# A list scheduler that counts VectorE's SBUF-only instructions and GpSimd's as exclusive, with a fixed part in each product's price

## The chip, the cores and the metric

The kernel runs on one core of a Trainium2 chip. The core has five engines with instruction streams of their own: TensorE (PE) for products, VectorE (DVE), ScalarE (ACT) and GpSimd (POOL) for elementwise work, SyncE (SP), whose queue issues all the DMAs here. The metric is the device time of one execution in microseconds, lower is better.

## The reference

One encoder layer is computed, for a prompt of 512 tokens (p) and a sample of 1024 tokens (s), 1024 features each, in float32. Cut to what matters:

```python
n = rms_norm(x, ln1_g) * (1 + sc1) + sh1
z = n @ w_in                                   # 1024 -> 2560
q, k, v, xl, gl = split(z)                     # 8 heads of 64, and 512 recurrent channels twice
att = neighbourhood_attention(rms_norm(q), rms_norm(k), v, rpb)    # 8 rows x 16 columns of a grid
xl = depthwise_conv(xl, lru_conv_w, lru_conv_b)
h = rg_lru(xl, forward) + rg_lru(xl, backward) # two linear scans over the tokens
x = x + g1 * (concat(att, h * gelu(gl)) @ w_out)
n2 = rms_norm(x, ln2_g) * (1 + sc2) + sh2
ug, uv = split(depthwise_conv(n2 @ w_up, ffn_conv_w, ffn_conv_b))  # 1024 -> 2 x 2816
x = x + g2 * ((gelu(ug) * uv) @ w_down)
```

The six modulation vectors (sh1, sc1, g1, sh2, sc2, g2) come from `silu(c) @ w_ada + b_ada`.

## The kernel before

The program is written as a recording: every call of `R.act`, `R.vec`, `R.tt`, `R.copy`, `R.mm`, `R.dma` makes an `Op` with an engine, a price in ns, the ops it depends on, and sometimes other engines that could do it (`alts`). Nothing is issued until `R.run()`. Then `_order` goes through all 14010 ops like a list scheduler: it keeps a clock for each engine, takes the engine whose next ready op can start first, gives that op a place in memory, moves the clock on by the op's price and hands the instruction out. The order of each engine's instructions, and the engine of each op that has a choice, come from the prices alone; the chip runs each engine's instructions in that order, with semaphores in between. Since all instructions are emitted from one line, nearly all rows of the profile say L351, and a tile is named by the arena that it was put in: `arena_f`, `arena_r` and `piece0` to `piece4` are SBUF memory (F as float32, R as float32r), `arena_s` holds small vectors, `bank` is a PSUM bank.

An op's key is the time by which it must start for TensorE to run without a halt; ready ops with a lower key go first. An op may be handed out only if it is less than a window (198 us of TensorE's priced work; 48 us for DMAs; other values in the up stage) ahead of the first op in program order that isn't done.

Ops with a choice are of two kinds. A copy (`act` with `either=True`, or `copy`, `ts` with `either=True`) can go to ScalarE or to DVE. A sum, difference or product of two SBUF tiles (`tt` with `pool=None`) can go to DVE or to POOL. When the engine that is free first takes such an op, `leave` asks whether another engine would be done with it sooner, its clock and the ready ops with lower keys counted in; in that question the op's own price is multiplied by a factor of the table `LEAN`, by its first engine and the engine that asks.

The stages: the norm, projections (768 rows of weights for q, k, v and the recurrence's two inputs at a time), the attention of each pair of heads and the recurrence, p first, then s; the output projection and second norm; up (`up`), each of 22 column blocks by Strassen's scheme in Winograd's form, 7 products instead of 8; down, in 5 chunks, by the same scheme. Every float32 operand of a product is split into a high part (a copy to float32r) and a low part (a difference), and a product is three (high x high, high x low, low x high). The scheme's terms (`s1` to `s4` of the left side, `t1` to `t4` of the right) are sums and differences with a choice between DVE and POOL; so are the low parts.

The recurrence's elementwise ops on a pair of heads of s have 1024 columns (`lru`): two products for each direction before the scan, one sum of the directions and one product with the gate, and two low parts of its input, all with a choice between DVE and POOL.

## Time and profile before

| | us |
|---|---|
| median of three timed runs | 1893.22 |
| lowest, highest | 1892.41, 1893.79 |
| span of the profiled execution | 1892.9 |
| TensorE busy | 1721.7 (91%) |
| VectorE busy | 1495.2 (79%) |
| ScalarE busy | 951.8 (50%) |
| GpSimd busy | 838.9 (44%) |

No other time is given for the profiled execution than its span, from the first to the last instruction. TensorE's busy time holds instructions that overlap in its pipeline and time that an instruction spent waiting inside it, so a busy TensorE is not one at its peak; a row's duration on DVE or POOL likewise holds the time that it was held up after its start. Shares over the whole span mix stages of different kinds, so the windows of single stages are of more use: on the time axis the projections and the attention lie at 0 to 640 us, the output projection and the second norm at 640 to 900, up at 800 to 1496, down at 1496 to the end, with its first sums and splits from 1443 on.

### The profile page before, as it was taken

The numbers are of one execution on the slowest core, as the hardware profiler recorded it, in microseconds if no ns is written. First come the engines' busy times: TensorE is split into PE (matmuls) and PEld (weight loads), VectorE is DVE, ScalarE is ACT, GpSimd is POOL, SyncE is SP. The second block draws the span as 40 slices with busy tenths as digits, with TensorE's granted clock in tenths as the row PEclk, the third lists the DMA queues.
The fourth block names the chain that finished last, engine by engine and source line by source line (L and its number), as shares of the span: only waits on it lengthen the run. The fifth ranks groups of instructions, "written<-read, shape, count | busy, mean of one in ns | idle before, by whom it ended". The sixth has DMA issues, their size and how long they took to land. (4 is left out here: it accounts for less than half of the span.)

```text
span 1892.9 us, 26075 instructions
## 1 busy us (share of the span) xinstructions
PE 1721.7 (91%) x8906; PEld 1416.1 (75%) x8906; DVE 1495.2 (79%) x2662; ACT 951.8 (50%) x1753; POOL 838.9 (44%) x656
## 2 busy tenths in 40 slices
PE   6987979989898899897999999999999888888978
PEld 3665767768687578797888888888887666776756
DVE  5697797897969874868767767667698998789998
ACT  3365863857676741454444444444454554243332
POOL 0364332362616321334333333333255776467874
PEclk9998989999999899998999999999999999999989
DMA  9435314040406465462122221221232331324322
GB/s 369 162 101 150 123 45 134 17 163 13 167 12 189 99 195 173 139 206 79 56 71 64 62 68 62 62 73 56 66 97 81 115 106 55 95 71 143 118 97 97
DMA packets 144695, 201.12 MB, mean 106 GB/s; under 512 B 15793, under 2 KB 83505, under 8 KB 144561
## 3 DMA queue, kind: packets, MB, share of 16 engines
q1 hardware_dynamic: 144560, 199.44, 33.2%
q8 instruction: 70, 1.15, 0.3%
q14 instruction: 65, 0.52, 0.1%
HBM read 157.97 MB, written 41.44 MB: 105 GB/s over the span
## 5 line engine op out<-in xcount | busy, mean ns | idle before, releaser
L351 PE MATMUL bank<-arena_r 128*128 128x512 f32 (+3 forms) x3487 | 859.6, 379 | 58.0 <-ACT piece0F L351 11.0
L351 PEld LDWEIGHTS bank<-arena_r 128*128 128x128 f32 (+1 forms) x3487 | 632.2, 192 | 192.3 <-issue 22.0
L351 PE MATMUL bank<-arena_r,piece0R 128*128 128x512 f32 (+3 forms) x1323 | 325.2, 346 | 8.5 <-DVE piece4F L351 4.4
L351 PEld LDWEIGHTS bank<-arena_r,piece0R 128*128 128x128 f32 (+1 forms) x1323 | 230.6, 194 | 41.5 <-issue 6.3
L351 POOL TENSOR_TENSOR arena_r<-arena_f,arena_r 128x256 fp32r<-128x256 f32 (+4 forms) x172 | 189.8, 1113 | 159.1 <-ACT arena_r L351 74.1
L351 POOL TENSOR_TENSOR arena_f<-arena_f 128x512 f32<-128x512 f32 (+5 forms) x149 | 178.9, 1207 | 99.6 <-issue 42.9
L351 ACT ACTIVATE arena_r<-arena_f 128x256 fp32r<-128x256 f32 (+4 forms) x245 | 115.0, 495 | 130.8 <-PE bank L351 77.8
L351 PE MATMUL bank<-arena_r,piece2R 128*128 128x512 f32 (+1 forms) x735 | 179.5, 335 | 0.0
L351 DVE SCALAR_TENSOR_TENSOR arena_f<-bank,arena_s,arena_f 128x255 f32<-128x255 f32 (+2 forms) x308 | 157.5, 535 | 21.2 <-ACT arena_f L351 10.5
L351 ACT ACTIVATE arena_f<-arena_f,arena_s 128x384 f32<-128x384 f32 (+2 forms) x166 | 101.7, 619 | 84.7 <-DVE arena_s L351 54.4
L351 PEld LDWEIGHTS bank<-arena_r,piece2R 128*128 128x128 f32 x735 | 126.6, 190 | 16.4 <-POOL piece2R L351 0.2
L351 PE MATMUL bank<-arena_r,piece4R 128*128 128x256 f32 (+1 forms) x453 | 137.5, 330 | 0.4 <-DVE arena_f L351 0.4
L351 DVE TENSOR_TENSOR arena_f<-arena_f 128x512 f32<-128x512 f32 (+5 forms) x148 | 134.8, 919 | 3.7 <-ACT arena_f L351 2.5
L351 DVE TENSOR_TENSOR arena_r<-arena_f,arena_r 128x256 fp32r<-128x256 f32 (+5 forms) x143 | 123.8, 882 | 6.6 <-ACT arena_r L351 2.6
L351 ACT ACTIVATE arena_f<-bank 128x512 f32<-128x512 f32 (+3 forms) x186 | 82.3, 454 | 75.1 <-DVE bank L351 36.9
L351 PE MATMUL bank<-piece0R,arena_r 128*128 128x512 f32 (+3 forms) x316 | 104.4, 398 | 2.1 <-DVE arena_s L351 2.0
L351 ACT ACTIVATE piece0R<-arena_f 128x512 fp32r<-128x512 f32 (+2 forms) x78 | 48.9, 627 | 113.1 <-PE bank L351 92.5
L351 ACT ACTIVATE arena_f<-bank,arena_s 128x512 f32<-128x512 f32 (+1 forms) x132 | 89.6, 683 | 24.5 <-PE bank L351 15.2
L351 DVE TENSOR_TENSOR bank<-bank,arena_f 128x512 f32<-128x512 f32 (+1 forms) x89 | 52.3, 589 | 51.3 <-PE bank L351 32.8
L351 PEld LDWEIGHTS bank<-arena_r,piece4R 128*128 128x128 f32 x453 | 83.5, 190 | 9.3 <-issue 0.8
L351 ACT ACTIVATE piece2R<-arena_f 128x512 fp32r<-128x512 f32 x63 | 39.8, 631 | 89.9 <-PE bank L351 77.9
L351 DVE SCALAR_TENSOR_TENSOR arena_f<-arena_f,arena_s 128x511 f32<-128x511 f32 (+3 forms) x102 | 70.9, 696 | 17.4 <-ACT arena_f L351 15.4
(432 smaller groups left out, 3214.1 us busy)
## 6 DMA issues: line engine op xcount, KB each, us to landing
arena_f<-in_w_up_dram SPq DMA_DIRECT2D x96, 256.0 KB
gd<-arena_f SPq DMA_DIRECT2D x62, 256.0 KB
piece2F<-in_ada_dram SPq DMA_DIRECT2D x18, 512.0 KB
arena_f<-in_w_qkv_dram SPq DMA_DIRECT2D x24, 384.0 KB
arena_f<-gd SPq DMA_DIRECT2D x39, 192.0 KB
piece3F<-in_ada_dram SPq DMA_DIRECT2D x14, 512.0 KB
arena_f<-gd SPq DMA_DIRECT2D x46, 128.0 KB
arena_f<-in_ada_dram SPq DMA_DIRECT2D x8, 512.0 KB
```

Source lines behind the costliest of these rows:

```text
L351: fn(**{k: (v.real() if isinstance(v, View) else v) for k, v in kw.items()})
```

## The change

Four things change in the scheduler, and nothing in what is recorded. Comments and docstrings are dropped too, so that line numbers move by a few (L351 becomes L355).

1. A clock `port` is shared by POOL and DVE. Each op gets a set `port` of the engines on which it uses the shared clock: POOL always; DVE when the op's operands are all in SBUF, but not for `tensor_reduce` and `reciprocal`. An op that is handed out to such an engine starts no sooner than `port` and moves it to its own end.
2. `leave` compares ends without factors, the `port` clock counted in on both sides; the table `LEAN` is gone.
3. A float32r product is priced `n / 2.4 + 13.5` ns, at least 109, where it was `n / 2.4 + 2.5`.
4. The windows, `LEAD`, `LAG` and the memory steps stay.

```diff
-LEAN = {("DVE", "POOL"): 0.389, ("DVE", "DVE"): 0.536, ("ACT", "ACT"): 0.611, ("ACT", "DVE"): 1.869, ("DVE", "ACT"): 1.004}
+ONE_PORT = ("tensor_reduce", "reciprocal")
...
-    def op(self, eng, cost, emit, reads, writes, aset=None, lat=0.0, also=(), alts=(), move=0.0):
+    def op(self, eng, cost, emit, reads, writes, aset=None, lat=0.0, also=(), alts=(), move=0.0, port=False):
...
+        o.port = {"POOL"} if eng == "POOL" or "POOL" in alts else set()
+        if port:
+            o.port.add("DVE")
...
-        self.op("DVE", per * n + base + (60 if ps else 0), self._emit(getattr(self.nc.vector, name), kw), reads, w, alts=alts)
+        self.op("DVE", per * n + base + (60 if ps else 0), self._emit(getattr(self.nc.vector, name), kw), reads, w, alts=alts, port=not ps and name not in ONE_PORT)
...
-            self.op("DVE", *b, [in0, in1], [out], alts={"POOL": a} if pool is None else {})
+            self.op("DVE", *b, [in0, in1], [out], alts={"POOL": a} if pool is None else {}, port=not self._ps(out, in0, in1))
...
-            cost = max(64.0, n) / 2.4 + 2.5 if rhs.ap.dtype == F32R else max(214.0, n / 0.6)
+            cost = max(max(64.0, n) / 2.4 + 13.5, 109.0) if rhs.ap.dtype == F32R else max(214.0, n / 0.6)
...
         def leave(o, e, s):
-            """Whether another engine would be done with o before e."""
+
+            own = (max(s, port) if e in o.port else s) + o.alts[e][0]
             for f, (cost, _) in o.alts.items():
                 if f != e:
                     ahead = sum(ops[p].all[f][0] for c, p, v in ready[f] if c < o.key and not stale(c, p, v, f))
-                    if max(clock[f], s) + ahead + cost < s + LEAN[o.first, e] * o.alts[e][0]:
+                    if max(clock[f], s, port if f in o.port else s) + ahead + cost < own:
                         return True
...
+            if e in o.port:
+                s = max(s, port)
+                port = s + o.cost
```

How many ops with a choice go where, by stage of the program:

| stage | copies to ScalarE / DVE before | after | two-input ops to DVE / POOL before | after |
|---|---|---|---|---|
| projections, recurrence, attention | 260 / 220 | 301 / 179 | 138 / 186 | 145 / 179 |
| output projection, second norm | 58 / 42 | 64 / 36 | 54 / 34 | 53 / 35 |
| up | 298 / 16 | 237 / 77 | 131 / 163 | 185 / 109 |
| down | 345 / 50 | 377 / 18 | 275 / 266 | 244 / 297 |

In the first stage 19 of the ops that leave POOL have 1024 columns.

The order of POOL before, at the recurrence of the first pair of heads of s. The four rows of 128x1024 are two products ahead of the scans, the sum of the directions and the product with the gate; 128x384 are biases of the attention, 4x64 low parts of its values:

```order
L351 TENSOR_TENSOR arena_f<-piece2F,arena_f 128x384 x2
L351 TENSOR_TENSOR arena_r<-piece2F,arena_r 128x4x64 x2
L351 TENSOR_TENSOR arena_f<-arena_f 128x384
L351 TENSOR_TENSOR piece4F<-piece4F 128x1024
L351 TENSOR_TENSOR piece3F<-piece3F,piece2F 128x1024
L351 TENSOR_TENSOR piece2F<-piece2F,piece4F 128x1024
L351 TENSOR_TENSOR piece2F<-piece2F 128x1024
L351 TENSOR_TENSOR piece0R<-piece4F,piece0R 128x4x64 x2
```

POOL after the change, at the same place:

```order
L355 TENSOR_TENSOR piece4F<-piece2F,arena_f 128x384 x2
L355 TENSOR_TENSOR arena_f<-piece2F,arena_f 128x384 x2
L355 TENSOR_TENSOR arena_r<-piece4F,arena_r 128x512
L355 TENSOR_TENSOR arena_f<-piece4F,arena_f 128x384
L355 TENSOR_TENSOR piece0R<-piece2F,piece0R 128x4x64 x2
L355 TENSOR_TENSOR arena_r<-arena_f,arena_r 128x768
```

And DVE after the change, there; the four SCALAR_TENSOR_TENSOR rows are two products of the recurrence and its two scans, bank rows belong to the attention:

```order
L355 SCALAR_TENSOR_TENSOR piece3F<-piece2F,piece3F 128x1024
L355 SCALAR_TENSOR_TENSOR piece2F<-piece3F,piece2F 128x1024
L355 TENSOR_TENSOR piece3F<-piece3F,piece2F 128x1024
L355 TENSOR_TENSOR piece2F<-piece2F,piece3F 128x1024
L355 SCALAR_TENSOR_TENSOR piece2F<-piece2F,piece3F 128x1024
L355 SCALAR_TENSOR_TENSOR piece3F<-piece3F,piece2F 128x1024
L355 TENSOR_TENSOR arena_r<-bank_73,arena_r 128x3x128
L355 TENSOR_TENSOR piece2F<-piece2F,piece3F 128x1024
```

The recurrence's rows of 128x1024 have gone from POOL to DVE, in a row ahead of its scans; POOL goes on with the attention's biases and the splits of the next weights.

The DMA queue (SP) before, where down begins. `gd<-arena_f` stores a finished column block of up, `in_w_down_dram` are weights of down, `arena_f<-gd` are its left operands:

```order
L351 DMA gd<-arena_f 128x512 x4
L351 DMA arena_f<-in_w_down_dram 128x512 x3
L351 DMA arena_f<-gd 128x128 x3
L351 DMA arena_f<-in_w_down_dram 128x512
L351 DMA arena_f<-gd 128x128 x9
L351 DMA gd<-arena_f 128x512 x2
L351 DMA arena_f<-gd 128x128 x12
L351 DMA arena_f<-gd 128x2x128 x2
```

And after the change:

```order
L355 DMA gd<-arena_f 128x512 x3
L355 DMA arena_f<-in_w_down_dram 128x512 x2
L355 DMA gd<-arena_f 128x512
L355 DMA arena_f<-in_w_down_dram 128x512
L355 DMA gd<-arena_f 128x512
L355 DMA arena_f<-gd 128x128 x3
L355 DMA arena_f<-in_w_down_dram 128x512
L355 DMA arena_f<-gd 128x128 x7
```

Down's loads have moved back against up's stores: 45 of them stand ahead of up's last store before, 35 after.

## Rows read from the trace of the kernel before

**Rows 1.** The page's slices: busy tenths of two engines in 40 slices.

```profile
PE   6987979989898899897999999999999888888978
DVE  5697797897969874868767767667698998789998
```

**Rows 2.** Windows by stage: length; busy us of PE, PEld, DVE, ACT, POOL; clock; DMA.

```profile
50.00:640.00 590.00, 525.23 (x2809) 417.62 (x2809) 487.98 (x1120) 373.97 (x705) 250.09 (x195) 0.95 0.35 109
640.00:900.00 260.00, 235.00 (x1326) 202.84 (x1325) 188.43 (x290) 123.44 (x203) 83.18 (x46) 0.96 0.45 144
900.00:1395.00 495.00, 493.80 (x2834) 435.28 (x2833) 348.57 (x567) 234.32 (x411) 177.47 (x123) 1.00 0.22 67
1395.00:1496.00 101.00, 91.55 (x391) 74.87 (x390) 89.85 (x161) 50.18 (x102) 61.18 (x66) 0.93 0.28 86
1496.00:1690.00 194.00, 175.11 (x738) 137.41 (x736) 163.49 (x219) 86.11 (x169) 119.43 (x105) 0.99 0.28 86
1690.00:1893.00 203.00, 165.82 (x655) 128.93 (x655) 189.57 (x225) 65.57 (x137) 142.08 (x113) 0.93 0.34 111
```

**Rows 3.** TensorE's waits in 50:640: who, for whom, us in total, times, longest.

```profile
PE bank L351 <- DVE arena_r L351: 9.0, 9, 3.6
```

**Rows 4.** Timelines of POOL, DVE and PE at 403:414: start, us, instruction, [idle before].

```profile
403.69 5.54 POOL L351 TENSOR_TENSOR arena_r<-arena_f,arena_r 128x768 fp32r<-128x768 f32 x3 [0.95 <-DMA piece4F<-vds]
...
404.76 0.81 DVE L351 TENSOR_SCALAR arena_s<-arena_s 128x16 f32<-128x16 f32 x1
405.49 2.04 DVE L351 TENSOR_SCALAR arena_f<-arena_f,arena_s 128x384 f32<-128x384 f32 x1
407.45 1.81 DVE L351 TENSOR_SCALAR arena_s<-arena_s 128x16 int32<-128x16 int32 x1
...
413.39 0.16 DVE L351 TENSOR_TENSOR arena_s<-arena_s 128x16 f32<-128x16 f32 x1
...
413.52 1.01 PE L351 MATMUL bank<-arena_r,piece0R 128*128 128x256 f32 x3 [3.55 <-DVE arena_r L351]
```

**Rows 5.** Timelines of DVE and POOL: products of the recurrence, 128x1024, in 300:420.

```profile
348.78 1.23 DVE L351 TENSOR_TENSOR piece2F<-piece2F,piece4F 128x1024 f32<-128x1024 f32 x1 [1.17 <-ACT piece2F L351]
...
370.68 3.08 DVE L351 TENSOR_TENSOR piece3F<-piece3F,piece4F 128x1024 f32<-128x1024 f32 x1
...
369.37 3.31 POOL L351 TENSOR_TENSOR piece3F<-piece3F,piece2F 128x1024 f32<-128x1024 f32 x1 [7.46 <-DVE piece3F L351]
```

**Rows 6.** Timelines of POOL and DVE in down: side by side, then each alone.

```profile
1605.36 1.47 POOL L351 TENSOR_TENSOR arena_r<-arena_f,arena_r 128x384 fp32r<-128x384 f32 x1
1606.79 1.46 POOL L351 TENSOR_TENSOR arena_f<-arena_f,piece3F 128x384 f32<-128x384 f32 x1
...
1605.88 1.50 DVE L351 TENSOR_TENSOR arena_r<-arena_f,arena_r 128x512 fp32r<-128x512 f32 x1
...
1615.42 1.01 POOL L351 TENSOR_TENSOR piece2F<-piece0F,arena_f 128x384 f32<-128x384 f32 x1 [2.03 <-DVE arena_f L351]
...
1804.66 0.68 DVE L351 TENSOR_TENSOR arena_r<-piece1F,arena_r 128x512 fp32r<-128x512 f32 x1
```

**Rows 7.** A window in the middle of up, columns as in rows 2.

```profile
1000.00:1050.00 50.00, 50.00 (x289) 44.14 (x288) 32.58 (x52) 22.96 (x40) 15.68 (x11) 1.00 0.22 66
```

**Rows 8.** Groups by form on POOL: xcount | busy us, mean ns | idle before.

```profile
L351 POOL TENSOR_TENSOR piece2F<-piece2F,piece4F 128x1024 f32<-128x1024 f32 x4 | 10.5, 2616 | 30.9 <-ACT piece2F L351 13.5 <-DVE piece2F L351 11.7 <-DVE arena_s L351 5.6
...
L351 POOL TENSOR_TENSOR arena_f<-arena_f 128x512 f32<-128x512 f32 x80 | 117.5, 1469 | 69.6 <-issue 41.2 <-DVE arena_f L351 12.6 <-DVE arena_r L351 9.4
```

**Rows 9.** Groups by form: low parts of 128x128 on POOL and on DVE.

```profile
L351 POOL TENSOR_TENSOR arena_r<-arena_f,arena_r 128x128 fp32r<-128x128 f32 x38 | 21.8, 586 | 24.4 <-DVE arena_r L351 11.5 <-ACT arena_r L351 7.4 <-DMA piece3F<-in_tab_dram 4.6
...
L351 DVE TENSOR_TENSOR arena_r<-arena_f,arena_r 128x128 fp32r<-128x128 f32 x24 | 10.0, 444 | 0.1
```

**Rows 10.** Waits in 1395:1496, columns as in rows 3.

```profile
ACT arena_f L351 <- DVE arena_f L351: 10.5, 10, 3.1
...
PE bank L351 <- ACT arena_f L351: 8.4, 2, 4.3
```

More of the change, by code (lines that the diff above doesn't have):

```diff
@@ L208 @@
 class Op:
-    __slots__ = ("pos", "eng", "cost", "lat", "emit", "deps", "left", "users", "ready", "bufs", "aset", "start", "end", "vt", "done", "name", "alts", "all", "win", "ver", "key", "first", "move", "late", "strict")
+    __slots__ = ("pos", "eng", "cost", "lat", "emit", "deps", "left", "users", "ready", "bufs", "aset", "start", "end", "vt", "done", "name", "alts", "all", "win", "ver", "key", "first", "move", "late", "strict", "port")
 class Recorder:
@@ L372, in act @@
             alts["DVE"] = (1.045 * self._n(in_) + 127 if self._ps(in_) else 0.523 * self._n(in_) + 67, self._emit(self.nc.vector.tensor_copy, dict(out=out, in_=in_)))
-        self.op("ACT", cost, self._emit(self.nc.scalar.activation, kw), [in_, scale, bias], [out, accum_out], aset=SETS.get(func), alts=alts)
+        self.op("ACT", cost, self._emit(self.nc.scalar.activation, kw), [in_, scale, bias], [out, accum_out], aset=SETS.get(func), alts=alts, port=either and not self._ps(out, in_))
     def _act(self, out, in_, scale=None):
@@ L568, in _order @@
         aset = None
-        moved = 0.0
+        moved = port = 0.0
         tick = 0
```

## The prediction

> **What bounds the kernel now.** I read the page's slices first [rows 1], then stage windows [rows 2], then TensorE's waits [rows 3], then single instructions where waits gather [rows 4 to 6]. In the slices the reader is to see three parts: TensorE at 7 to 9 tenths with VectorE (DVE) at 7 to 9 in the first third, TensorE full in the middle, and TensorE falling to 7 or 8 at the end while DVE stands at 9. The windows give them numbers [rows 2]. In 50:640 (projections, recurrence, attention) TensorE is idle for 590 - 525.23 = 65 us and its granted clock is 0.95 of full speed; DVE is busy for 487.98 us, 83%. In 900:1395 (up products) TensorE is busy for 493.80 of 495: that stretch can't be shortened by any order. In 1395:1496 it idles 9 us, in 1496:1690 19 us, in 1690:1893 37 us; there DVE is busy for 189.57 of 203 us, 93%. So order and division of work decide outside 900:1395, through DVE. TensorE's longest wait in the first stretch, summed over one pair of tiles, is for DVE [rows 3].
>
> What DVE loses is visible too. At 403.69 three GpSimd (POOL) products of 128x768 run for 5.54 us, and a DVE instruction on 128x16 takes 1.81 us in that time, where a like one takes 0.16 us later; TensorE's 3.55 us of idle end right behind [rows 4]. Two products of 128x1024 side by side end 4.39 us after the first began (369.37 to 370.68 + 3.08), where one alone on DVE takes 1.23, two in a row some 2.46 [rows 5]. In the down stage POOL and DVE take turns, POOL starting every 1.43 us [rows 6]. So these two engines shut each other out on SBUF, and a planner that prices an instruction as if it were alone divides wrongly.
>
> **The change part by part.** *TensorE's price.* A 512-column product goes from 215.8 to 226.8 ns, one of 256 from 109.2 to 120.2 (from the formulas of the diff). The up stage is half of each: the new mean is 173.5 ns, and the trace shows 50 us for 289 products, 173 ns [rows 7]. The new price is right; by itself it moves no work between engines, and it shortens the planner's look ahead by 5 to 10% of products, since its windows are not changed. I cost that at nothing on its own; it is part of the term for the down stage below.
>
> *Projections and attention (50:640).* Here 19 products of 128x1024 of the sample's recurrence go from POOL to DVE, and 12 more small ones (net) go to POOL; 41 copies (net) go from DVE to ScalarE. POOL loses 19 x 2.616 = 50 us [rows 8], 20% of its 250.09 busy us [rows 2]. DVE takes 19 x 1.23 = 23 us [rows 5] and gives up some 41 copies and 12 products of roughly half a us each, an estimate from the 0.444 us of a 128x128 product and 0.68 us of a 128x512 one [rows 6, 9]: 26 us. Its own work stays. What it saves is waiting. Beside the 5.54 us of POOL at 403.69 it waits some 3.7 us (0.81 - 0.16, 1.81 - 0.16, and 2.04 less the 0.68 of a wider product), 0.66 of it [rows 4, 6]; in front of an instruction that reads PSUM, as many of DVE's are, it waits for nothing. I take 0.4 of POOL's time for the stretch: 0.4 x 50 = 20 us back, with 0 and 33 as bounds. TensorE is not behind DVE everywhere, so I take three quarters: **-15 us** (0 to -33). ScalarE gets 41 copies, at about 0.5 us some 20 us on 374 of 590: it stays the less busy engine, and if its cover is gone the cost is those 20 us at most.
>
> That figure can be weighed against the Trainium skill, SBUF — State Buffer, Who interferes with whom: the pair of ports that VectorE and GpSimd share is a lock held for the whole instruction, and the second one fully blocks. The trace has 1.43 us for a pair whose parts alone are 0.68 and 1.01 us [rows 6], so about a quarter us overlaps, and here the measurement decides. By the page's whole lock the share would be nearer the 0.66 above, the term -25, and the sum below 1870.
>
> *640:900.* Out projection and second norm: of 188 instructions with a choice 6 more go to ScalarE and 1 more to POOL, net; TensorE idles 25 us [rows 2]. I take -2, with 6 either way.
>
> *Up, 900:1395.* 61 copies go from ScalarE to DVE and 54 products from POOL to DVE: at most 115 x 0.68 = 78 us more on DVE's 348.57, so 86% of 495 instead of 70%, while POOL gives up 54 x 1.469 = 79 us of its 177 [rows 2, 6, 8]. TensorE has no idle time to win and hides this as long as DVE keeps up: 0, and up to +10 if it does not.
>
> *The end of up, 1395:1496.* TensorE waits twice, for 8.4 us together, for ScalarE, which itself waits for DVE there [rows 10]. In this stretch the old order already does down work (below); the new one does less of it, so the stretch gets lighter: -4 (0 to -9).
>
> *The start of down, 1496:1690.* In the order in which the planner hands instructions out, 63 DVE and 50 POOL instructions of the down stage stand ahead of the last up product; after the change 11 and 21. The DMA queue says the same: 45 loads of the down stage stand ahead of up's last store before, 35 after. So 52 DVE and 29 POOL instructions move behind the last product of up, most of them 128x128: 52 x 0.444 = 23 us of DVE and 29 x 0.586 = 17 us of POOL [rows 9]. DVE is busy for 163.49 of 194 us there [rows 2], idle for 30.5. 23 us fit, and part of the 17; but at the start TensorE waits for just this work. Bounds 0 and +40; I take **+8**, nearer to the end at which idle time takes it.
>
> *The rest of down, 1690:1893.* In the whole down stage 31 products (net) go from DVE to POOL, and 32 copies from DVE to ScalarE. With DVE at 93% this looks like relief, but a POOL product keeps the ports longer than a DVE one (1.01 us for 384 columns against 0.68 for 512, [rows 6]), so what 31 DVE products free goes to waiting: 0, with 8 us either way.
>
> *Sum* against the profiled execution's own span: 1892.9 - 15 - 2 + 0 - 4 + 8 + 0 = **1880 us**. The median of the three timed runs, 1893.22, is 0.3 us from that span, so I carry the sum over as it is.
>
> **The rivals.** *Down starts cold (slower).* All 40 us of DVE and POOL work that the new order leaves behind the last up product come on top, because the ports are full in the down stage: DVE at 93% in its second half speaks for it, and that the planner, told of the ports, still gives POOL 297 of 541 products there, where it gave 266. Against it stands the 16% of idle DVE in 1496:1690. With -15 and -4 kept: 1892.9 - 19 + 40 = 1914, and 1905 if a quarter of it finds room. It decides once DVE can no longer take up the first 20 of the 40 us, that is, once it is busy for over 94% between up's last product and the middle of down.
>
> *A truer order gains more.* The term of the first stretch prices only moved instructions. Here the planner also knows that DVE is late, and puts what TensorE waits for ahead of the rest. If a third of the 65 us of idle goes and the granted clock rises with it (a mean of 0.95 with levels of 1.2 and 2.4 GHz is a tenth of the 590 us, 59 us, at the low one, which costs up to 30 us): -22 - 10 on top, 1848. For it: DVE's waits of 1 to 2 us on tiny instructions [rows 4]. Against: POOL's work there shrinks by a fifth only.
>
> *Nothing that can be measured.* The change does not do what its price says: POOL still takes most products in down, DVE's own work is the same in the first stretch, and what is won there is lost at the start of down: 1889 to 1897.
>
> **How the numbers follow.** I give the forecast (1862 to 1889) 0.40, the truer order 0.17, no change 0.13, the cold start 0.30. A measurement of this kernel tells some 0.2% from no change, 3.8 us; the cases give faster 0.57, same 0.13, slower 0.30. The range takes in the truer order's 1848 and most of the cold start: 1846 to 1912. The forecast's own range, from the bounds of its terms, is 1862 to 1889.
>
> **What would show it.** In the changed profile: no 128x1024 product of the recurrence on POOL, POOL's busy time down to some 210 us before 640 us, and the up stage's end some 15 to 20 us earlier on the time axis: right for the first term. TensorE's idle time in the first 25 to 50 us of down larger than now, and DVE near 95% there: the cold start. If TensorE is below 98% in the middle of up, DVE did not keep up there, and my 0 for that stretch is wrong. The prediction fails if the first stretch keeps its 65 us of idle, or if down loses more than 20 us.

## The result, and the profile after

The changed kernel takes 1847.1 us (median of 4 runs, 1845.4 to 1850.9) where the kernel before takes 1893.5: a ratio of 0.976, 95% interval 0.9746 to 0.9774, so 46 us less. The direction was forecast, the size was not: the forecast was 13 us less, with a range that just reaches down to the measured time. The rival that gave 1848, a truer order, had been given 17%. Of the kernel with one number changed (1840.1 us, below) one run in four took 3331.7 us, and the time given is the median of the other three.

The page of the changed kernel, against [rows 1] and the table of busy times of before; TensorE is fuller in the first tenth and behind the middle, GpSimd emptier until down begins, and DVE at 9 tenths in two of the last 13 slices where it was in six:

```profile
PE 1716.7 (93%) x8906; PEld 1411.1 (76%) x8906; DVE 1436.9 (78%) x2673; ACT 944.2 (51%) x1769; POOL 720.5 (39%) x627
...
PE   7998879899999699999999999999999889998878
...
DVE  5676878877988775878687777777787888879889
...
POOL 0244233061616200336221111111133689968877
```

To compare stage by stage, both traces are cut where TensorE has got through the same amount of work (its products, each at the new price, in the order in which they ran), at the moments that are 50, 640, 900, 1395, 1496 and 1690 us before. Windows of the changed kernel at those cuts, with the columns of [rows 2]:

```profile
47.70:609.40 561.70, 517.51 (x2810) 414.17 (x2809) 443.40 (x1066) 389.33 (x750) 211.26 (x202) 0.96 0.34 107
609.40:866.20 256.80, 238.05 (x1328) 203.26 (x1327) 189.95 (x298) 125.59 (x209) 67.08 (x41) 0.95 0.52 164
866.20:1367.80 501.60, 497.31 (x2835) 436.60 (x2833) 371.52 (x692) 202.10 (x350) 86.88 (x64) 1.00 0.22 65
1367.80:1455.60 87.80, 86.84 (x390) 71.09 (x389) 65.18 (x105) 43.40 (x82) 38.07 (x33) 1.00 0.23 72
1455.60:1649.60 194.00, 176.36 (x737) 140.18 (x736) 166.02 (x223) 103.92 (x225) 159.53 (x154) 0.96 0.34 102
1649.60:1846.90 197.30, 166.23 (x655) 127.31 (x653) 175.16 (x211) 64.29 (x134) 155.34 (x129) 0.94 0.34 113
```

The lengths of these windows less those of before, beside the terms of the forecast. At 1690 TensorE of the kernel before stands in a wait that ends at 1692.5; the table counts it to the stretch ahead of the cut, which is then 196.4 us long, and the last one 200.4:

| stage, by the times of before | forecast (bounds) | measured |
|---|---|---|
| ahead of 50 | none | -2.3 |
| 50:640 projections, recurrence, attention | -15 (0 to -33) | -28.5 |
| 640:900 output projection, norm | -2 (±6) | -3.2 |
| 900:1395 up | 0 (up to +10) | +6.5 |
| 1395:1496 end of up | -4 (0 to -9) | -13.1 |
| 1496:1690 start of down | +8 (0 to +40) | -2.4 |
| 1690 to the end | 0 (±8) | -3.1 |
| sum | -13 | -46 |

So the gain is in the first stretch and at the end of up, and over the whole start of down nothing is lost. In the first stretch TensorE idles 561.7 - 517.5 = 44 us instead of 65, and its busy time is 8 us shorter. At the end of up it idles 1 us instead of 9, at a granted clock of 1.00 instead of 0.93. The two waits of 8.4 us together there [rows 10] are gone; TensorE's waits in 1367.8:1455.6 (columns as in [rows 3]):

```profile
PE bank L355 <- DVE piece2R L355: 0.5, 1, 0.5
PE bank L355 <- ACT arena_f L355: 0.4, 1, 0.4
```

Inside the start of down a loss is there, and is won back. Two pieces of equal work, first in the kernel before, then in the changed one: the first of them takes 7.9 us longer, with TensorE idle for 10 us instead of 6 and at a lower granted clock, the second 7.5 us less, since TensorE has no wait left in it:

```profile
1503.40:1552.80 49.40, 43.42 (x179) 32.30 (x178) 46.02 (x73) 30.64 (x66) 38.27 (x39) 1.00 0.39 118
1552.80:1600.50 47.70, 41.44 (x178) 32.69 (x177) 41.88 (x50) 19.69 (x37) 28.14 (x21) 1.00 0.24 73
...
1461.70:1519.00 57.30, 47.01 (x179) 34.38 (x179) 49.85 (x68) 42.52 (x103) 49.04 (x59) 0.94 0.34 104
1519.00:1559.20 40.20, 40.20 (x178) 32.98 (x177) 34.16 (x51) 22.50 (x46) 35.07 (x34) 1.00 0.46 138
```

**One place, close up.** What a plan without the turns does is to be seen at 100 us in the kernel before. TensorE stops for 4.76 us; first its timeline, then VectorE's and GpSimd's up to that moment:

```profile
105.17 0.69 PE L351 MATMUL bank<-arena_r,piece1R 128*128 128x384 f32 x1 [4.76 <-DVE arena_f L351]
```

```profile
97.49 2.13 DVE L351 CAST arena_r<-arena_f 128x256 fp32r<-128x256 f32 x2
99.54 0.41 DVE L351 TENSOR_TENSOR arena_r<-arena_f,arena_r 128x256 fp32r<-128x256 f32 x1
99.88 2.64 DVE L351 CAST arena_r<-arena_f 128x768 fp32r<-128x768 f32 x2
102.44 2.15 DVE L351 CAST arena_r<-piece2F 128x768 fp32r<-128x768 f32 x1
104.51 0.41 DVE L351 COPY piece3F<-bank 128x256 f32<-128x256 f32 x1
104.84 0.27 DVE L351 COPY arena_f<-bank 128x128 f32<-128x128 f32 x1
```

```profile
99.70 1.93 POOL L351 TENSOR_TENSOR arena_r<-arena_f,arena_r 128x768 fp32r<-128x768 f32 x1 [0.50 <-DVE arena_r L351]
102.12 2.05 POOL L351 TENSOR_TENSOR arena_r<-arena_f,arena_r 128x768 fp32r<-128x768 f32 x1 [0.49 <-DVE arena_r L351]
104.67 1.82 POOL L351 TENSOR_TENSOR arena_r<-piece2F,arena_r 128x768 fp32r<-128x768 f32 x1 [0.50 <-DVE arena_r L351]
```

TensorE needs its bank emptied: the copies at 104.51 and 104.84. Ahead of them VectorE works from 97.49 to 104.59 on six splits of weights, which TensorE wants only for products further on (in the changed kernel they run 15 us and more behind the copy). The planner put them there because by its prices they end 2.4 us after they begin (70.3 to 72.7 on its own clock). They take 7.1, since the long casts stand still while GpSimd works on SBUF too: the one at 102.44 ends at 104.59, 0.42 us after the GpSimd product that began ahead of it (102.12 + 2.05). In the changed order five of the six are ScalarE's and one GpSimd's, behind the copy, which comes at 87.56. ScalarE's rows and VectorE's copy in the changed kernel:

```profile
103.50 2.33 ACT L355 ACTIVATE arena_r<-arena_f 128x768 fp32r<-128x768 f32 x3
...
106.10 0.86 ACT L355 ACTIVATE arena_r<-arena_f 128x768 fp32r<-128x768 f32 x1
```

```profile
87.56 0.42 DVE L355 COPY piece2F<-bank 128x256 f32<-128x256 f32 x1 [0.95 <-PE bank L355]
```

The Trainium skill, SBUF — State Buffer, Who interferes with whom, says that VectorE in a two-port mode, which a cast can take, contends with GpSimd: whoever issues first has the shared ports for the whole instruction, and the other fully blocks. This place agrees: 2.15 us for a cast of 128x768 that starts behind a GpSimd product of 2.05.

### The profile page after: what moved, and what is told of

Its sections match the earlier page's. It is cut to its first block, busy times and chain, and to the rows that moved or that the text cites. A ratio compares the mean times of both kernels' runs of the same rounds, so it can differ in the third digit from the quotient of the medians.

```text
span 1846.9 us, 25865 instructions
## 1 busy us (share of the span) xinstructions
PE 1716.7 (93%) x8906; PEld 1411.1 (76%) x8906; DVE 1436.9 (78%) x2673; ACT 944.2 (51%) x1769; POOL 720.5 (39%) x627
## 5 line engine op out<-in xcount | busy, mean ns | idle before, releaser
L355 PE MATMUL bank<-arena_r 128*128 128x512 f32 (+3 forms) x4042 | 979.9, 373 | 58.0 <-ACT arena_r L355 13.5
L355 PEld LDWEIGHTS bank<-arena_r 128*128 128x128 f32 (+1 forms) x4042 | 716.6, 192 | 201.2 <-issue 26.2
L355 POOL TENSOR_TENSOR arena_f<-arena_f 128x512 f32<-128x512 f32 (+5 forms) x181 | 196.2, 1091 | 462.0 <-DVE arena_f L355 195.3
L355 POOL TENSOR_TENSOR arena_r<-arena_f,arena_r 128x256 fp32r<-128x256 f32 (+4 forms) x174 | 194.0, 1128 | 164.1 <-ACT arena_r L355 107.4
L355 PE MATMUL bank<-arena_r,piece4R 128*128 128x512 f32 (+1 forms) x868 | 215.4, 340 | 0.3 <-DVE piece4R L355 0.3
L355 ACT ACTIVATE arena_r<-arena_f 128x256 fp32r<-128x256 f32 (+5 forms) x276 | 131.8, 507 | 141.0 <-PE bank L355 80.7
L355 PE MATMUL bank<-arena_r,piece0R 128*128 128x384 f32 (+4 forms) x772 | 186.1, 362 | 3.9 <-ACT piece3F L355 1.3
L355 DVE SCALAR_TENSOR_TENSOR arena_f<-bank,arena_s,arena_f 128x511 f32<-128x511 f32 (+2 forms) x306 | 156.7, 535 | 22.7 <-ACT arena_f L355 15.1
L355 PEld LDWEIGHTS bank<-arena_r,piece4R 128*128 128x128 f32 x868 | 148.5, 190 | 18.2 <-DVE piece4R L355 0.7
L355 PEld LDWEIGHTS bank<-arena_r,piece0R 128*128 128x128 f32 (+1 forms) x772 | 131.6, 194 | 35.7 <-issue 10.1
L355 ACT ACTIVATE arena_f<-bank 128x256 f32<-128x256 f32 (+3 forms) x197 | 86.8, 445 | 138.2 <-DVE bank L355 70.1
L355 ACT ACTIVATE arena_f<-arena_f,arena_s 128x384 f32<-128x384 f32 (+3 forms) x164 | 99.2, 610 | 86.7 <-DVE arena_f L355 70.9
L355 DVE TENSOR_TENSOR arena_r<-arena_f,arena_r 128x384 fp32r<-128x384 f32 (+5 forms) x146 | 121.3, 840 | 16.7 <-ACT arena_r L355 15.8
L355 PE MATMUL bank<-piece0R,arena_r 128*128 128x512 f32 (+5 forms) x430 | 130.0, 373 | 0.1
L355 ACT ACTIVATE arena_f<-bank,arena_s 128x512 f32<-128x512 f32 (+1 forms) x135 | 92.3, 689 | 67.4 <-PE bank L355 56.9
L355 DVE TENSOR_TENSOR arena_f<-arena_f 128x512 f32<-128x512 f32 (+5 forms) x124 | 96.4, 788 | 13.6 <-ACT arena_f L355 11.3
L355 PEld LDWEIGHTS bank<-piece0R,arena_r 128*128 128x128 f32 (+1 forms) x430 | 75.7, 188 | 16.1 <-issue 3.6
L355 POOL TENSOR_TENSOR piece0R<-piece2F,piece0R 128x256 fp32r<-128x256 f32 (+2 forms) x17 | 16.9, 997 | 171.4 <-ACT piece0R L355 89.6
L355 ACT ACTIVATE piece2F<-bank,arena_s 64x512 f32<-64x512 f32 (+1 forms) x76 | 53.7, 719 | 43.7 <-PE bank L355 28.6
L355 DVE TENSOR_TENSOR bank<-bank,arena_f 128x512 f32<-128x512 f32 (+1 forms) x88 | 51.3, 586 | 23.4 <-PE bank L355 14.9
```

What stands on the lines that cost most here:

```text
L355: fn(**{k: (v.real() if isinstance(v, View) else v) for k, v in kw.items()})
```

## Experiments: the three parts, each alone and in pairs

Three theories stood at the start. DIVISION, the forecast's: fewer instructions on GpSimd, so VectorE waits less. ORDER, the rival's: the planner knows what is late. PRICE: TensorE's new price does it. The change has three separable parts, the turns (`port`), the price and the removal of the factors (`LEAN`).

**Price alone** (the kernel before with):

```diff
-            cost = max(64.0, n) / 2.4 + 2.5 if rhs.ap.dtype == F32R else max(214.0, n / 0.6)
+            cost = max(max(64.0, n) / 2.4 + 13.5, 109.0) if rhs.ap.dtype == F32R else max(214.0, n / 0.6)
```

> The kernel before with one part of the change alone: TensorE's new price (a 512-column product planned at 226.8 ns instead of 215.8). Factors and everything else as before. Three theories for the 46 us. DIVISION (which engine does an instruction makes the gain, by GpSimd's share): the price leaves GpSimd's planned work nearly as it was (213 to 198 us in the projections, attention and recurrence, 241 to 240 in down), so within 5 us of 1893. ORDER (the planner knows of the two engines' turns and so of lateness): the price alone tells it nothing of these, 1885 to 1895. PRICE (a TensorE that is planned 5 to 10% slower shortens the look ahead and moves every deadline): most of the gain is here, 1850 to 1870.

Measured 1906.6 us, ratio 1.0068 (1.0046 to 1.0091): slower, by 0.7%. PRICE falls, and no theory had it slower.

**Turns alone** (`o.port` and the clock `port` as in the change, `own` and the ends of `leave` with `port`, but the factor kept in `own`, and the old price):

```diff
-            own = (max(s, port) if e in o.port else s) + o.alts[e][0]
+            own = (max(s, port) if e in o.port else s) + LEAN[o.first, e] * o.alts[e][0]
```

> The kernel before with one part of the change alone: VectorE's SBUF-only instructions and GpSimd's take turns in the plan. The old factors and TensorE's old price stay. With the factors kept, GpSimd is given MORE planned work than before (213 to 279 us in projections, attention and recurrence, 51 to 77 in the stretch behind it, 200 to 218 in up, 241 to 272 in down). DIVISION: more GpSimd work makes VectorE wait more, so slower than before, 1900 to 1930. ORDER: the plan is truer, so faster in spite of it, 1860 to 1880. PRICE: nothing, 1888 to 1898.

Measured 1865.1 us, ratio 0.9847 (0.983 to 0.9864). ORDER holds, DIVISION falls. GpSimd works more than before in the first stretch, 312.73 us against 250.09 [rows 2], and the stretch is 28 us shorter. Its window at the same cuts:

```profile
48.20:609.90 561.70, 515.66 (x2814) 415.08 (x2812) 423.29 (x968) 400.06 (x777) 312.73 (x263) 0.95 0.35 110
```

**Factors gone alone** (no turns, old price):

```diff
-                    if max(clock[f], s) + ahead + cost < s + LEAN[o.first, e] * o.alts[e][0]:
+                    if max(clock[f], s) + ahead + cost < s + o.alts[e][0]:
```

> The kernel before with one part of the change alone: the five factors are gone, an instruction goes to the engine that would be done first. No turns in the plan, TensorE's old price. GpSimd's planned work falls more than in the full change (213 to 145 us in projections, attention and recurrence, 200 to 127 in up, 241 to 217 in down). DIVISION: most of the gain, 1855 to 1870. ORDER: little, 1885 to 1900. PRICE: nothing, 1888 to 1898.

Measured 1874.6 us, ratio 0.990 (0.9885 to 0.9915): 19 us, more than ORDER allowed and less than DIVISION asked. In the first stretch it gains 2 us; the rest is spread over the later stages. It moves the same 19 recurrence products as the full change.

**All but the price.** 

> The changed kernel with TensorE's old price put back: the turns are in the plan and the factors are gone. DIVISION: GpSimd's planned work is 174 us in the first stages and 255 in down, as in the full change (170, 258): 1845 to 1860. ORDER: the turns are there: 1845 to 1865. PRICE: the gain goes, 1875 to 1895.

Measured 1861.0 us, ratio 0.9835 (0.981 to 0.986), 14 us behind the full change.

**Turns and price, factors kept.** 

> The changed kernel with the five old factors put back: turns in the plan and TensorE's new price. The theory now is CLOCK: a plan is as good as its own clock is true, because the planner decides by it what is late. In the three kernels run so far whose plan has both the turns and the new price, the plan's end and the profiled span stand close to 61 us apart (plan 1785.8, 1787.6, 1856.5; medians 1847.1, 1849.3, 1918.3). The end of this plan is 1809.3. CLOCK: 1809.3 + 61.6 = 1871, within 5. Rival SUM (the three parts add up): 1893.7 + 12.4 for the price - 28.6 for the turns = 1877.5, within 5; a rival by which the factors are what holds the price back: 1895 or more.

Measured 1863.8 us, ratio 0.9845 (0.983 to 0.986): 7 us below what CLOCK (below) gave, 14 below the plain sum.

**Price and no factors, no turns.** 

> The changed kernel without the turns: TensorE's new price, no factors. With it all eight combinations of the three parts have been run. CLOCK: the plan's clock still runs away from the chip's (the plan ends at 1665.6), so nothing like 1847: 1870 to 1900. SUM: 1893.7 + 12.4 - 19.1 = 1887. DIVISION (GpSimd's planned work in the first stages is the smallest of all here, 126 us): below 1870.

Measured 1915.7 us, ratio 1.0124 (1.0107 to 1.0141). All three expectations missed: it is slower than either part alone. Medians of all eight, in us:

| | old price, factors | old price, no factors | new price, factors | new price, no factors |
|---|---|---|---|---|
| no turns | 1893.5 (before) | 1874.6 | 1906.6 | 1915.7 |
| turns | 1865.1 | 1861.0 | 1863.8 | 1847.1 (after) |
| the turns give | -28 | -14 | -43 | -69 |

The turns are worth 14 to 69 us whatever else is there. The price costs 13 and 41 us without turns, and gains 1 (within the noise) and 14 with them. How long VectorE's instructions are held up doesn't decide, as far as one group tells: the largest group of its 128x512 products (128x512 into `arena_f`, mean ns behind the comma) in the kernel before, with turns alone (28 us faster), and with price and no factors (22 us slower):

```profile
L351 DVE TENSOR_TENSOR arena_f<-arena_f 128x512 f32<-128x512 f32 x80 | 84.7, 1063 | 3.4 <-ACT arena_f L351 2.5 <-DMA arena_f<-in_w_down_dram 0.2
```

```profile
L356 DVE TENSOR_TENSOR arena_f<-arena_f 128x512 f32<-128x512 f32 x78 | 83.6, 1074 | 3.1 <-ACT arena_f L356 1.3 <-POOL arena_f L356 1.3
```

```profile
L353 DVE TENSOR_TENSOR arena_f<-arena_f 128x512 f32<-128x512 f32 x74 | 58.6, 811 | 0.9 <-ACT arena_f L353 0.3
```

The faster of the two is the one that is held up more.

## Experiments: who does it, and in what order

Four kernels carry a list that fixes the engine of each of the 2536 ops with a choice, and let either planner make the order:

```diff
+        who = iter(WHO)
+        for o in ops:
+            o.who = None if len(o.all) == 1 else {"D": "DVE", "P": "POOL", "A": "ACT"}[next(who)]
...
-            o.alts = dict(o.all)
+            o.alts = dict(o.all) if o.who is None else {o.who: o.all[o.who]}
```

> Every instruction stays on the engine that the kernel before gives it (a list in the kernel says which), and only the order is made by the changed planner: turns of VectorE and GpSimd in the plan, TensorE's new price. The 925 instructions that the change moves to another engine are not moved. ORDER: 1855 to 1870, most of the 46 us. DIVISION: within 8 us of 1893. If new hands and new order are each half of it: about 1870.

> Every instruction goes to the engine that the changed kernel gives it (a list in the kernel says which), 925 of them another than before, and the order is made by the planner of before: each priced as if it were alone, TensorE at the old price. ORDER: within 8 us of 1893, or slower. DIVISION: 1850 to 1865. If each is half of it: about 1870.

> A gauge: the engines of before and the planner of before, engines given by the list. Nothing is changed but that an instruction is offered to one engine instead of two or three, which shuffles the order a little (222 of 2566 VectorE instructions stand elsewhere). Any theory: 1893, and by how much it is off tells what a shuffle of no intent moves; I expect up to 8 us either way.

> A gauge of the same kind: the engines and the planner of the changed kernel, engines given by the list (481 of 2577 VectorE instructions stand elsewhere). Any theory: 1847, up to 8 us either way. With the three others it makes a table of hands by order whose four kernels are built alike.

| | order by the planner before | order by the changed planner |
|---|---|---|
| engines of before | 1895.6, ratio 1.0004 (0.9992 to 1.0016) | 1918.3, 1.0135 (1.0114 to 1.0155) |
| engines of after | 1924.6, 1.0155 (1.0138 to 1.0172) | 1849.3, 0.9764 (0.9741 to 0.9787) |

ORDER and DIVISION both fall in their pure form: either half alone costs 25 to 31 us, both together give 44. The two gauges stay within 2.2 us of the kernels that they copy, though 222 and 481 VectorE instructions stand elsewhere in them, so a shuffle without intent moves little. The gain needs engines and order of the same plan; that it is the common clock that makes them fit is the reading tested next.

## Experiments: is it the planner's clock?

The planner keeps a start time for every instruction. The trace's start of a TensorE instruction less the planned one, at equal TensorE work (at the new prices; the end is 1609 us of work, and up runs from 644 to 1294), shows how far that clock is off, in us:

| | at 100 | 500 | 700 | 1200 | 1300 | end |
|---|---|---|---|---|---|---|
| before | 51 | 148 | 187 | 222 | 243 | 331 |
| price alone | 41 | 130 | 162 | 164 | 181 | 258 |
| factors gone alone | 48 | 137 | 162 | 197 | 216 | 294 |
| price, no factors | 40 | 118 | 134 | 143 | 163 | 243 |
| turns alone | 19 | 69 | 80 | 110 | 116 | 114 |
| all but the price | 19 | 74 | 83 | 119 | 123 | 116 |
| turns and price | 15 | 56 | 58 | 60 | 64 | 53 |
| after | 21 | 69 | 66 | 67 | 69 | 59 |

Without turns the clock runs away wherever VectorE and GpSimd decide, in the first stretch and in down; with the old price it runs away in up, 30 to 36 us between 700 and 1200. With both it is off by some 60 us, nearly all of it before 500, and then it keeps time. Hence the theory CLOCK: the planner decides by its clock what is late, and a clock that keeps time decides well.

The table alone does not bear that out. Among the four kernels without turns the two whose clock is less far off at the end are the slower ones (258 and 243 us off: 1906.6 and 1915.7 us; 331 and 294 off: 1893.5 and 1874.6), and turns and price with the factors kept has the least error, 53, at 1863.8. What the table shows is which part of the change removes which error; that a truer clock is worth time is shown only where the turns are added, four times out of four.

**The same end without turns.** The changed kernel without `port`, but VectorE's SBUF-only instructions and GpSimd's priced 1.65 times as long:

```diff
+        o.all = {e: (c * 1.65 if e in busy else c, f) for e, (c, f) in o.all.items()}
```

> The changed kernel without the turns, but with VectorE's SBUF-only instructions and GpSimd's planned 1.65 times as long, so that its plan ends at the same time as that of the changed kernel (1785.0 against 1785.8). CLOCK as the turns: the plan's mean is right but not the instruction that waits, so worse than 1847 by 20 us or more: 1865 to 1900. Rival SLACK: any plan that thinks VectorE late puts its work in time, so 1840 to 1860.

Measured 1882.6 us, ratio 0.9929 (0.9905 to 0.9953): SLACK falls, CLOCK's forecast holds. The plan ends where the changed kernel's does and the kernel is still 36 us slower. At equal work its clock is 19, 69, 74, 82, 87 and 99 us off in the columns of the table, less at the end than with turns alone (114), which is 18 us faster: so a right mean is not enough. That it matters which instruction the plan holds up is a reading, since this plan also puts 692 of the 2536 ops with a choice on another engine than the changed kernel. Its product of the group above takes 817 ns, the changed kernel's 779:

```profile
L358 DVE TENSOR_TENSOR arena_f<-arena_f 128x512 f32<-128x512 f32 x89 | 71.3, 817 | 13.5 <-ACT arena_f L358 13.0
```

```profile
L355 DVE TENSOR_TENSOR arena_f<-arena_f 128x512 f32<-128x512 f32 x91 | 70.2, 779 | 13.5 <-ACT arena_f L355 11.3 <-POOL arena_f L355 0.5 <-DMA gd<-arena_f 0.5
```

**Turns in some stages only.**

```diff
+        if o.pos >= 5865:
+            o.port = set()
```

> The changed kernel with the turns only in the stages up to the second norm; the up and down stages are planned without them. CLOCK by stages: the first stretch as in the changed kernel (36 us ahead of before at equal TensorE work of 700 us), and from there on what the kernel without any turns loses, some 20 us: about 1877. If the first stretch makes the whole gain: 1845 to 1855.

> The complement: turns only from the up stage on. CLOCK by stages: the first stretch as in the kernel without turns (level with before at equal TensorE work of 700 us, 1 us ahead), from there on as the changed kernel, which gains some 10 us more: about 1884. If the end of up and the down stage make the whole gain: 1845 to 1860.

Measured 1880.6 us (ratio 0.9931, 0.9908 to 0.9953) and 1882.0 (0.9938, 0.9919 to 0.9957), by CLOCK 1877 and 1884. The first gains 30 us in 50:640 and loses 5 at the end of up and 11 in the last stretch; the second loses 9 in 50:640 and gains 12 at the end of up and 15 behind it. Against the kernel before that is 13 and 12 of the 46 us; against the kernel that has everything but the turns (1915.7) it is 35 and 34, together the 69 that turns throughout give. So the gain goes with the turns, stage by stage.

**Why the price hurts without turns.** The kernel with price, no factors and no turns, its windows and its lag made 1.06 times as long:

```diff
-WINDOW = {"PE": 198e3, "ACT": 198e3, "DVE": 198e3, "POOL": 198e3, "DMA": 48e3}
+WINDOW = {"PE": 209.9e3, "ACT": 209.9e3, "DVE": 209.9e3, "POOL": 209.9e3, "DMA": 50.9e3}
```

> The kernel with the new price, no factors and no turns (1915.7 us), with its windows of look ahead and its lag made 1.06 times as long, so that they hold as many products as with the old price. LOOK AHEAD: back to the kernel with the old price, 1874.6, so 1870 to 1885. RELATIVE PRICE (the plan now thinks TensorE slower beside a VectorE whose waits it doesn't know): it stays where it was, 1905 to 1925. In between, both.

Measured 1907.1 us, ratio 1.0064 (1.0044 to 1.0084): of the 41 us the shorter look ahead explains some 9. What is left points to the relative price: TensorE too cheap and VectorE too cheap may be two errors that partly cancelled, so that mending the first alone makes VectorE look early. That reading is by exclusion; no run shows it by itself.

**The forecast's first term alone.** The kernel before, with the recurrence's two products, its sum and its product with the gate barred from GpSimd where they have 1024 columns (16 of the 20 ops of that width that GpSimd had; of the four low parts it keeps three). One of four such lines:

```diff
-            R.tt(i, i, xc, ALU.mult, pool=None)
+            R.tt(i, i, xc, ALU.mult, pool=None if nT == 512 else False)
```

> The kernel before with the forecast's first term alone: the products of the sample's recurrence (128x1024, four places in the code) may not go to GpSimd. Everything else as before; the old planner makes the order. GpSimd's planned work in the first stages goes from 213 to 174 us, VectorE's from 391 to 407. FORECAST: its term of -15 us (0 to -33): 1879. CLOCK: the plan's clock still knows no turns, so no gain that lasts: 1885 to 1900.

Measured 1895.7 us, ratio 1.0003 (0.9985 to 1.0021): nothing. GpSimd's busy time in the first stretch fell as the forecast said, from 250.09 [rows 2] to 218.34, and the stretch is not shorter but 4 to 8 us longer, by whether the group of products at its end (from 641.5 on) is counted to it. Its window:

```profile
47.00:644.90 597.90, 530.33 (x2815) 418.14 (x2814) 494.71 (x1123) 377.27 (x714) 218.34 (x183) 0.94 0.35 109
```

**A plan with an earlier end.** If the clock is right, the planner can be asked for a better plan. A search over its windows, lag and factor on times ahead, by the planned end alone, gave two kernels. First one number, the look ahead of loads in up (82e3 to 40173 ns), then six:

```diff
-WINDOW_UP = {"PE": 44e3, "ACT": 115e3, "DVE": 115e3, "POOL": 115e3, "DMA": 82e3}
-BEST, LEAD, LAG = True, 1.275, 19e3
+WINDOW_UP = {"PE": 27864.0, "ACT": 41180.0, "DVE": 41180.0, "POOL": 41180.0, "DMA": 40173.0}
+BEST, LEAD, LAG = True, 1.131, 22.4e3
...
-WINDOW = {"PE": 198e3, "ACT": 198e3, "DVE": 198e3, "POOL": 198e3, "DMA": 48e3}
+WINDOW = {"PE": 198e3, "ACT": 198e3, "DVE": 198e3, "POOL": 198e3, "DMA": 48540.0}
```

> The changed kernel with one number changed: in the up stage a load may be put in order 40.2 us of TensorE's work ahead of the program's place, instead of 82. The number was found by looking for the earliest end of the plan. The plan ends at 1754.9, 30.9 us before that of the changed kernel. CLOCK: 1754.9 + 61.6 = 1816.5, within 8. Rival CHANCE (plans of one kind differ by what the planner can't see, and the earliest of many is the luckiest): within 10 of 1847.

> The changed kernel with six numbers of the planner changed to those with the earliest end of the plan that a search by the plan's own clock found: look ahead in the up stage 27.9 us (products), 41.2 (ScalarE, VectorE, GpSimd) and 40.2 (loads) instead of 44, 115 and 82, of loads elsewhere 48.54 instead of 48, the factor on times ahead 1.131 instead of 1.275, the lag 22.4 instead of 19 us. The plan ends at 1733.8, 52 us before that of the changed kernel. CLOCK: 1733.8 + 61.6 = 1795, within 10. CHANCE: 1835 to 1855.

Measured 1840.1 us (ratio 0.9716, 0.970 to 0.9732) and 1805.5 (0.9534, 0.952 to 0.9548). The first missed CLOCK's 1816.5 by 24 us and lies within CHANCE's range; the second missed 1795 ± 10 by half a us and is far from CHANCE. It beats both kernels, by 88 and 42 us. The six plans with turns and new price, by planned end: 1733.8, 1754.9, 1785.8, 1787.6, 1809.3, 1856.5; measured: 1805.5, 1840.1, 1847.1, 1849.3, 1863.8, 1918.3. The order is right throughout, the distance lies between 54 and 85 us. So among plans with turns and new price the planned end ranks the kernels (not across kinds: 1785.0 without turns gave 1882.6), and an early end found by search kept 42 of 52 us once and 7 of 31 the other time. Where the first kernel's clock broke is to be seen in up, 880:1360: the plan has TensorE run through, the trace has 16 short waits for VectorE.

```profile
PE bank L355 <- DVE arena_f L355: 13.0, 16, 1.0
```

The fastest kernel's windows at the same cuts, from 50 on: 24.6 us less than before at the start of down (against 196.4), 14 at the end of up, 41 in the first stretch.

```profile
45.10:594.10 549.00, 509.99 (x2810) 413.71 (x2809) 445.65 (x1065) 382.78 (x736) 216.98 (x201) 0.96 0.36 113
...
1354.60:1441.30 86.70, 86.11 (x391) 71.11 (x390) 75.52 (x133) 50.48 (x111) 51.50 (x67) 1.00 0.35 108
1441.30:1613.10 171.80, 168.69 (x738) 137.52 (x736) 151.22 (x205) 91.30 (x186) 139.23 (x119) 1.00 0.32 99
```

## Why the prediction was right in direction and wrong in size

*What bounds the kernel.* Right: VectorE decides outside the middle of up, and the two engines shut each other out on SBUF. All that was gained lies in stretches that the forecast had named as open. Some lines were read too fast: the slices of DVE run from 5 to 9 in the first third and from 7 to 9 at the end, and TensorE's wait of 3.55 us [rows 4] begins at 409.97, when the three GpSimd products shown are over (409.23) and three others are under way.

*TensorE's price.* Right as a number (173 ns mean in [rows 7]), wrong as an effect. "I cost that at nothing on its own": alone it costs 13 us, within the full change it gains 14. So it has no effect of its own that could be added; that this is because a price changes what every other engine's lateness is measured against is argued, not shown.

*Projections and attention.* This is the step that failed: -15 us, priced as the waiting that VectorE is spared by 19 products fewer on GpSimd. The stretch became 28.5 us shorter, and none of it by that. "What it saves is waiting", 0.4 of the 50 us that 19 products take on GpSimd: the products did leave (of 20, one is left there; `piece2F<-piece2F` below), GpSimd's busy time before 640 us came out at 218, near the 210 named, and none of that is the gain. In its place stands the turns clock, by which engines and order are chosen anew throughout: 925 ops are on another engine, where the forecast's net counts had 19, 12 and 41 in this stretch. Those products barred from GpSimd alone give nothing, and turns alone, with 19 of the 20 still there, give the whole 28 us. The one such row of the changed kernel:

```profile
L355 POOL TENSOR_TENSOR piece2F<-piece2F 128x1024 f32<-128x1024 f32 x1 | 2.4, 2403 | 0.5 <-ACT piece2F L355 0.5
```

That the term's bounds reached -33 was luck of the arithmetic, not of the mechanism: the bound is 0.66 of 50 without the three quarters that the term has, and with them it is -25, short of what was measured. The weighing of the whole-lock rule, which would have made the term -25, was therefore about the wrong quantity, though its number is nearer. Its reading of [rows 6], by which the measurement speaks against a whole lock, does not hold either (last section).

*640:900 and up.* -3.2 for -2, and +6.5 for 0 with +10 as the bound. Up lost its 6.5 us in the first 100 us of work: the lead over before is 36 us at 700 of work, 28 at 800, and the same 28 at 1200. In the rest of up VectorE kept up, as forecast.

*The end of up.* -13.1 for -4, outside the bounds 0 to -9. The sign of the mechanism was right (down's early work makes way); the term took only the idle time, and left out that the granted clock there rises from 0.93 to 1.00, and the same products are busy for 86.84 us instead of 91.55. Up's end comes 41 us earlier than before, where the text looked for 15 to 20.

*The start of down.* -2.4 for +8. In the first piece shown above 7.9 us are lost, which is the term; that it is lost for what was left behind fits, but no run shows it. Missed was the piece behind it, where the waits of the old order are gone and 7.5 us come back. VectorE is busy for 166.02 of 194 us, 86%, below the 94% from which the cold start was to decide; that rival, with 30%, falls, though its sign came in part: in the first 50 us TensorE is idle for 9 us instead of 7, with VectorE at 88%. (Its 1905 should be 1904 by its own sum.)

*The rivals.* "A truer order gains more" was right in kind and in the working of its own term: a third of the 65 us of idle, 22, measured 21; 10 for the clock, measured 8 of busy time, at a granted clock of 0.96 instead of 0.95. But it set these on top of the -15, so 47 us in the first stretch, where 28.5 were measured; that its total of 1848 met the time to 1 us is luck, since the 18.5 too much there are made up by what came elsewhere, 17.6 less where its sum has 2 more. What spoke against it, that GpSimd's work shrinks by a fifth only, was no argument: with turns alone it grows. It should have been the forecast, since the diff changes a clock by which every choice is made, not 19 choices; the few ops that moved were weighed because they could be counted.

*The range.* 1846 took in the measured time for the rival's sake. The forecast's own 1862 to 1889 does not come out of the bounds of its terms, though the text says so: 1862 is the first term at -33 with the others as they stand.

*What stays open.* Why the planner chooses better with turns is shown by stage, not down to the instruction, and CLOCK as a number missed: by 7 us with the factors kept, by 16 without turns, by 24 for the one changed number. Why the engines of after under the old order lose 31 us in up, and why the old engines under the new order lose 22 in 640:900 (at a granted clock of 0.90 there, where it was 0.96), was not followed further. Nor was the 60 us by which even the best clock is off at the start.

## What to carry to other kernels

A change of a planner's prices is not the sum of the instructions that it moves: compare the planner's own clock with the trace first, stage by stage, and look where the two part. Try corrections together as well as alone: here the true price of TensorE's products cost 13 to 41 us alone and gained up to 14 once the turns were in. Once the clock keeps time, it can be used to search for a better plan, and the winner should be expected to fall short of its promise by the clock's own scatter (the measured times lie 54 to 85 us behind the plans, 61 for the kernel that the search began with).

## What the hardware showed that was not expected

A VectorE instruction on SBUF that starts behind one of GpSimd's does nearly all of its work after that one has ended, a cast as well as a product. The 128x768 cast at 102.44 took 2.15 us where the planner has 0.47; a like one at 101.97, with no GpSimd product running at its start, took 0.55. It ended 0.42 us after the GpSimd product beside it, so all but 0.13 of its own time came then. The 128x512 product at 1605.88 [rows 6] ends 0.55 us after the GpSimd product of 1605.36, and takes 0.68 alone: again all but 0.13. In the whole trace of the kernel before, 182 of VectorE's products of 128x512 on SBUF start inside a GpSimd product and at least 0.3 us ahead of its end; 180 of them end 0.55 us after it, to 0.03. The quarter of a us by which the pair of [rows 6] is shorter than its parts is thus this first 0.13 of each of the two. A copy from a bank was not held up: the one at 104.84, inside a GpSimd product that runs from 104.67 on, took 0.27 us.

And a product's fixed part is not small: 512 and 256 columns in equal numbers take 173 ns on average [rows 7]. The Trainium skill (TensorE: Matmul & The Clock Gate, Back-to-back issue gap) gives N / 2.4 + 2.5 as the warm gap of a single product, which is the old price and makes an estimate of 162.5 ns; the trace has 10.5 more, and the measurement decides. So small an error made the planner's clock lose 30 us in up, between 700 and 1200 us of work, with turns alone.
